# Strassen's block products for 16 of 22 input blocks of a down projection, with weight sums made by accumulating transfers

## The chip, the cores and the metric

One core of a Trainium2 chip runs the kernel. The metric is the device time of one execution in microseconds (us), the median of several. The engines are named as the profile names them: PE is TensorE's matmuls and PEld its weight loads (here the stationary operand of a matmul, which in this stage is an activation tile), DVE is VectorE, ACT is ScalarE, POOL is GpSimd and SP is SyncE. SP and POOL each issue transfers on a queue of their own.

## What is computed

A transformer-like block over 512 tokens of width 1024: an SSD branch and an attention branch are merged and added to x, and then comes a gated feed-forward network, whose last line is what the change is about.

```python
x = x + merged @ w_out[l]
h2 = rms_norm(x, norm2_g[l])
u = causal_dwconv(h2 @ w_up[l], ffn_conv_w[l], ffn_conv_b[l])
u_gate, u_val = jnp.split(u, 2, axis=-1)
x = x + (jax.nn.silu(u_gate) * u_val) @ w_down[l]
```

All inputs are float32. `w_down` is 2816 x 1024, so the down projection multiplies 512 x 2816 activations by it: 22 input blocks of 128 channels, two column halves of 512, four token tiles of 128.

## The kernel before

Every float32 operand of a product is split into a high part (`hi`, rounded to the matmul's format) and a low part (`lo`, the rest). A product of two blocks is then three matmuls: high x high, low activation x high weight, high activation x low weight.

Weights come in pieces of 512 KB in the order of a list, `pieces`. `load_piece` (L90) issues the load of the next on SP into one of three `raw` buffers; `make_piece` (L96) has ACT copy it to `whi` (L105) and DVE subtract to `wlo` (L106), three buffers each. A buffer is free when PE has done with the piece that held it. For the down projection a piece is two input blocks by one column half, `[128, 2, 512]`.

The activations stand in `act`, 22 blocks of `[128, 512]`, channels on partitions and tokens along the row. `split_act` (L1257) makes the high part on ACT and the low part on DVE, into `pre` for the first two blocks and into `asp` for the rest.

The up projection runs before, one block m of 22 after the other (loop at L1265). Its even blocks from 4 on (`fast`) already take Strassen's 7 products, with sums of weights made on POOL (`form`) and sums of activations in `sh`, `sl`. The last block, m = 21, is a plain one: 48 matmuls. During it the first two pieces of the down projection are loaded and made, and the first two activation blocks are split.

After it come the convolution of block 21 (`conv_a` on ACT, `conv_s` on DVE), its silu and product (`mul`, L1160), the load of the residual x into `x1b` (2 MB, L1376), and the down projection: `mm_tok` (L946) once for each column half. It takes four PSUM banks, one for each token tile, goes through the 11 pieces, and issues 24 matmuls for each: 4 token tiles x 3 terms x 2 blocks, with the activation tile `[128, 128]` stationary and the weights `[128, 512]` moving (L952). The last two pieces of a half are taken tile by tile, so that each bank ends at a time of its own; `store` then adds it into `x1b` on DVE (L1384) and SP stores 256 KB (L1385). The activations are split a second time for the second half.

PE's instructions are issued in the order written throughout. For DVE, ACT and POOL the written order holds from L1167 to the exit of `up_cm` at L1370; after it a planner sets the order. Each engine takes its instructions in order.

SBUF is two stacks. On the left, `pre` stays below `sums` (`sh`, `sl`, 32 KB a partition), `wx` and `gu`; on the right `down` takes the place of `h2` and `x1b` comes after it. A tile that takes another's place waits for that one's last reader.

Of the kernel before, what the change touches and what calls it, by code (L numbers as in the profile page):

```python
# [8 lines left out]
F32 = mybir.dt.float32  # L9
F32R = mybir.dt.float32r  # L10
AF = mybir.ActivationFunctionType
ALU = mybir.AluOpType
# [4 lines left out]
P = 128  # L17
# [17 lines left out]
NF = DFF // P  # L35
# [3 lines left out]
def kernel(  # L39
# [6 lines left out]
    nc = tc.nc  # L46
    x, out = x[0], out[0]
    w_in, w_ssd_proj, w_attn_proj, w_out, w_up, w_down = (
        w[0] for w in (w_in, w_ssd_proj, w_attn_proj, w_out, w_up, w_down))
# [4 lines left out]
    def pool(name, side="left", bufs=1):  # L54
        return tc.tile_pool(name=name, bufs=bufs, side=side, reuse_waits="tile")

    cp = ctx.enter_context(pool("const"))
    wp = ctx.enter_context(pool("weights"))
# [3 lines left out]
    def bank(tag, name):  # L62
        return pp.tile([P, 512], F32, tag=tag, name=name, bufs={"mm": 4, "tr": 2, "aux": 2}[tag])


    def chan_piece(w, c0, n, k0=0, nk=KD):
        return w[k0 * P:(k0 + nk) * P, c0:c0 + n].rearrange("(k p) c -> p k c", p=P)

    pieces = []
# [12 lines left out]
    pieces += [chan_piece(w_out, n * 512, 512, k, 2) for n in range(2) for k in range(0, KD, 2)]  # L82
    first_up = len(pieces)
    pieces += [chan_piece(w_up, i * DFF + m * P, P) for m in range(NF) for i in range(2)]
    pieces += [chan_piece(w_down, n * 512, 512, k, 2) for n in range(2) for k in range(0, NF, 2)]
    raws, made = [], []
    used = [0]
    marks = {}
# [1 line left out]
    def load_piece():  # L90
        n = len(raws)
        raw = wp.tile([P, pieces[n].shape[1], pieces[n].shape[2]], F32, tag="raw", name=f"raw{n}", bufs=3)
        nc.sync.dma_start(raw, pieces[n])
        raws.append(raw)

    def make_piece():  # L96
        n = len(made)
        if n == len(pieces):
            return
        if n == len(raws):  # L100
            load_piece()
        raw, shape = raws[n], list(raws[n].shape)
        hi = wp.tile(shape, F32R, tag="whi", name=f"whi{n}", bufs=3)
        lo = wp.tile(shape, F32R, tag="wlo", name=f"wlo{n}", bufs=3)
        nc.scalar.copy(hi, raw)  # L105
        marks["lo"] = nc.vector.tensor_sub(lo, raw, hi.bitcast(F32))  # L106
        made.append((hi, lo))

    def prefetch(n=2):
        while len(made) < min(used[0] + n, len(pieces)):  # L110
            make_piece()

    def next_piece(ahead=1):
        i = used[0]
        used[0] += 1
        while len(made) < min(i + 1 + ahead, len(pieces)):
            make_piece()
        return made[i]
# [690 lines left out]
    for g in range(8):  # L809
# [4 lines left out]
        banks = []  # L814
        for i in range(6):
            w = next_piece()
# [61 lines left out]
    for m2 in range(4):  # L878
        w = next_piece()
        for j in range(2):  # L880
            m = 2 * m2 + j
            ps = bank("mm", f"ps_ap{m}")
# [9 lines left out]
    with pool("ysplit") as sp:  # L892
# [14 lines left out]
        for m4 in range(2):  # L907
            pss = [bank("mm", f"ps_sp{m4}_{j}") for j in range(4)]
            for k2 in range(8):
                hi, lo = next_piece()  # L910
                ys = split_y(8 * m4 + k2)
                split_y(8 * m4 + k2 + 1)
                for j in range(4):
                    if j == 2:
                        prefetch()
                    cs = slice(j * P, (j + 1) * P)
                    for i, (w, xi) in enumerate(((hi, 0), (hi, 1), (lo, 0))):
                        for k in range(2):
                            nc.tensor.matmul(pss[j], w[:, k, cs], ys[k][xi],  # L919
                                             start=(k2 == 0 and i == 0 and k == 0),  # L920
                                             stop=(k2 == 7 and i == 2 and k == 1))
# [13 lines left out]
    act = actp.tile([P, NF, S], F32, tag="act", name="act")  # L935
# [10 lines left out]
    def mm_tok(xs, nk, name, fin, last, ahead=lambda k: None):  # L946
        pss = [bank("mm", f"ps_{name}{b}") for b in range(NT)]

        def part(b, k0, w):
            for j, (ww, i) in enumerate(((w[0], 0), (w[0], 1), (w[1], 0))):  # L950
                for k in range(2):
                    nc.tensor.matmul(pss[b], xs(k0 + k, i)[:, b * P:(b + 1) * P], ww[:, k, :],  # L952
                                     start=(k0 == 0 and j == 0 and k == 0),
                                     stop=(k0 == nk - 2 and j == 2 and k == 1))
        for k0 in range(0, nk - 2 * last, 2):
            w = next_piece()
            for b in range(NT):
                part(b, k0, w)
                if b == 1:
                    ahead(k0 + 2)  # L960
                    prefetch()
        ws = [next_piece(0) for i in range(last)]
        for i in range(1, last):
            ahead(nk - 2 * last + 2 * i)

        def ending(b):
            for i, w in enumerate(ws):
                part(b, nk - 2 * last + 2 * i, w)
            return pss[b]
        if fin is None:  # L970
            return ending
        prefetch(1)
        for b in range(NT):
            fin(b, ending(b))
# [3 lines left out]
    sums = n2.tile([P, NT, 2], F32, tag="sums", name="sums")  # L978
# [43 lines left out]
    H = 256  # L1022
# [116 lines left out]
    def conv_a(m, i):  # L1139
        if 0 <= m < NF:  # L1140
            if i == 0:
                facc[m] = gu.tile([P, S], F32, tag="facc", name=f"facc{m}", bufs=1)
            blk = m + NF * i
            nc.scalar.activation(act[:, m, :] if i else facc[m], (ga, ua)[i][m], AF.Identity,
                                 bias=sc[:, FB + blk:FB + blk + 1], scale=sc[:, FW + 88 + blk:FW + 89 + blk])
# [12 lines left out]
    def mul(m):  # L1158
        if 0 <= m < NF:
            nc.vector.tensor_mul(act[:, m, :], act[:, m, :], facc[m])  # L1160
# [6 lines left out]
    up_cm = tc.manual_schedule(engines={mybir.EngineType.DVE, mybir.EngineType.Activation, mybir.EngineType.Pool})  # L1167
# [9 lines left out]
    ps = ending(2)  # L1177
# [7 lines left out]
    ps = ending(3)  # L1185
# [69 lines left out]
    asp = {}  # L1255

    def split_act(k, p, tag, bufs):  # L1257
        t = p.tile([P, 2, S], F32R, tag=tag, name=f"{tag}{len(asp)}_{k}", bufs=bufs)
        nc.scalar.copy(t[:, 0, :], act[:, k, :])
        nc.vector.tensor_sub(t[:, 1, :], act[:, k, :], t[:, 0, :].bitcast(F32))  # L1260
        return t
# [3 lines left out]
    for m in range(2, NF):  # L1265
# [7 lines left out]
        else:  # L1273
            pss = [bank(t, f"ps_u{m}_{i}") for i, t in enumerate(("aux", "tr"))]
# [73 lines left out]
            asp[1] = split_act(1, pre, "pre", 2)  # L1348


    m = NF - 1
    h2_cm.__exit__(None, None, None)
    dn_cm = pool("down", side="right")
    dn = dn_cm.__enter__()
    fresh = {0, 1}

    def ahead(k):
        for i in (k, k + 1):
            if i < NF and i not in fresh:
                asp[i] = split_act(i, dn, "asp", 8)  # L1360
                fresh.add(i)

    ahead(2)
    conv_a(m, 1)
    conv_a(m, 0)
    conv_s(m, 1)
    conv_s(m, 0)
    silu_g(m)
    mul(m)
    up_cm.__exit__(None, None, None)  # L1370
    gu_cm.__exit__(None, None, None)
    wx_cm.__exit__(None, None, None)
    ss_cm.__exit__(None, None, None)
    xb_cm = pool("x1b", side="right")
    x1b = xb_cm.__enter__().tile([P, NT, D], F32, tag="x1b", name="x1b")
    nc.sync.dma_start(x1b, x1d.rearrange("(t p) d -> p t d", p=P))  # L1376

    def xs_a(k, i):
        return asp[k][:, i, :]

    def store(nh):
        def fin(b, ps):
            cs = slice(nh * 512, (nh + 1) * 512)
            nc.vector.tensor_add(x1b[:, b, cs], x1b[:, b, cs], ps)  # L1384
            nc.sync.dma_start(out[b * P:(b + 1) * P, cs], x1b[:, b, cs])  # L1385
        return fin

    mm_tok(xs_a, NF, "wd0_", store(0), 2, ahead)
    fresh.clear()
    ahead(0)  # L1390
    mm_tok(xs_a, NF, "wd1_", store(1), 2, ahead)
    xb_cm.__exit__(None, None, None)
    dn_cm.__exit__(None, None, None)
    pre_cm.__exit__(None, None, None)
    act_cm.__exit__(None, None, None)
# [28 lines left out]
```

## Time and profile before

| | |
|---|---|
| median of 3 runs | 1204.27 us (1204.27 to 1204.46) |
| the profiled execution | 1204.23 us, of which the span is 1202.3 us |
| PE busy | 1196.1 us of the span |
| DVE, ACT, POOL busy | 753.7, 575.4, 170.5 us |
| bytes moved | 138.95 MB, 116 GB/s on the mean |

The span goes from the first instruction to the last. "Busy" counts the time in which an engine has at least one instruction under way. In a list of groups, each row has the line of the kernel, the engine, the operation, the tile written and the tiles read, their shapes and the count; then busy time, the mean duration in ns, the idle time of the engine just before these instructions, and what ended most of it. In a list in order of time, a row starts with the start and the length in us.

### The profile page before, as it was taken

To read this page: it belongs to the slowest core of one execution; us is meant where nothing else is said; L and a number is where in the kernel's file an instruction comes from. 1 tells how busy PE (TensorE), PEld (TensorE's weight loads), DVE (VectorE), ACT (ScalarE), POOL (GpSimd) and SP (SyncE) were. 2 spreads that over 40 slices of the span, in tenths; PEclk is the share of its full clock that TensorE was granted. 3 is DMA by queue.
4 is the path that set the end of the run, shared out by engine and by line. 5 is a ranking of instruction groups with operands and counts; after the bars stand their busy time and mean duration, and the time that the engine had idled before them with its cause. 6 is when DMAs were issued, how large, how long until landed. Compare 5 with 4: busy or idle time off the path is not lost.

```text
span 1202.3 us, 15963 instructions
## 1 busy us (share of the span) xinstructions
PE 1196.1 (99%) x6316; PEld 997.8 (83%) x6316; DVE 753.7 (63%) x999; ACT 575.4 (48%) x890; POOL 170.5 (14%) x143
## 2 busy tenths in 40 slices
PE   9999999999999999999999999999999999999998
PEld 7877778987888888888888888888888989988887
DVE  6224544467789986877644354654788887885542
ACT  5434565467845657456433324433554445454331
POOL 1034422300000201101011000000223232400000
PEclk9999999999999999999999999999999999999999
DMA  5455544322646444434325332344333332334330
GB/s 187 123 124 128 114 103 107 91 66 74 184 124 200 122 134 124 123 97 115 87 72 144 119 103 90 105 142 157 123 108 103 105 107 85 109 95 168 112 116 35
DMA packets 174955, 138.95 MB, mean 116 GB/s; under 512 B 11552, under 2 KB 149584, under 8 KB 173857
## 3 DMA queue, kind: packets, MB, share of 16 engines
q1 hardware_dynamic: 172001, 131.35, 37.6%
q0 software_dynamic: 2880, 6.59, 2.4%
q8 instruction: 49, 0.80, 0.3%
q14 instruction: 25, 0.20, 0.1%
HBM read 133.22 MB, written 4.70 MB: 115 GB/s over the span
## 4 chain that ended last, share of the span: by engine, by line
PE 99%; ACT 0%; DVE 0%; issue 0%; POOL 0%; DVEq 0%
PE ps_ssd L145 22%; PE ps_qk L145 11%; PE ps_u L1282 10%; PE ps_wd L952 10%; PE ps_gate L145 7%; PE ps_sp L919 7%; PE ps_v L409 6%; PE ps_wo L952 3%; PE ps_ua L1108 2%; PE ps_uc L1108 2%; PE ps_ub L1108 2%; PE ps_u L145 2%; PE ps_ap L145 2%; PE ps_s L537 1%; PE ps_y L764 1%; PE ps_pv L579 1%
## 5 line engine op out<-in xcount | busy, mean ns | idle before, releaser
L106 DVE TENSOR_TENSOR wlo<-raw,whi 128x1024 fp32r<-128x1024 f32 x154 | 194.3, 1263 | 315.2 <-ACT whi L105 217.1
L105 ACT CAST whi<-raw 128x1024 fp32r<-128x1024 f32 x154 | 161.7, 1051 | 308.3 <-PE ps_ssd L145 63.1
L145 PE MATMUL ps_ssd<-hl,whi 128*128 128x512 f32 x384 | 102.9, 397 | 0.0
L145 PE MATMUL ps_ssd<-hh,whi 128*128 128x512 f32 x384 | 98.4, 398 | 0.0
L145 PE MATMUL ps_ssd<-hh,wlo 128*128 128x512 f32 x384 | 95.4, 390 | 0.0
L952 PE MATMUL ps_wd<-whi,asp 128*128 128x512 f32 x336 | 89.8, 389 | 0.0
L145 PEld LDWEIGHTS ps_ssd<-hh,wlo 128*128 128x128 f32 x384 | 72.1, 188 | 15.9
L145 PEld LDWEIGHTS ps_ssd<-hh,whi 128*128 128x128 f32 x384 | 70.6, 188 | 14.0 <-issue 0.2
L145 PEld LDWEIGHTS ps_ssd<-hl,whi 128*128 128x128 f32 x384 | 70.2, 188 | 14.1 <-issue 0.2
L952 PEld LDWEIGHTS ps_wd<-whi,asp 128*128 128x128 f32 x336 | 63.1, 188 | 13.1
L952 PE MATMUL ps_wd<-wlo,asp 128*128 128x512 f32 x168 | 51.7, 389 | 0.0
L556 ACT ACTIVATE s<-s,st 128x128 f32<-128x128 f32 (+1 forms) x96 | 39.8, 417 | 21.6 <-DVE st L550 15.7
L145 PE MATMUL ps_qk<-hh,whi 128*128 128x512 f32 x192 | 49.3, 398 | 0.0
L1156 ACT ACTIVATE facc<-facc 128x512 f32<-128x512 f32 x22 | 13.9, 632 | 71.7 <-DVE facc L52 71.6
L145 PE MATMUL ps_qk<-hl,whi 128*128 128x512 f32 x192 | 47.4, 389 | 0.0
L145 PE MATMUL ps_qk<-hh,wlo 128*128 128x512 f32 x192 | 47.4, 389 | 0.0
L1092 DVE TENSOR_TENSOR ulo<-rawup,uhi 128x1024 fp32r<-128x1024 f32 x31 | 43.5, 1404 | 5.2 <-ACT uhi L1086 5.2
L778 POOL TENSOR_TENSOR sq<-sq 128x512 f32<-128x512 f32 x8 | 12.4, 1550 | 240.5 <-ACT sq L775 240.5
L145 PEld LDWEIGHTS ps_qk<-hh,whi 128*128 128x128 f32 x192 | 35.0, 188 | 12.1 <-issue 3.8
L1282 PE MATMUL ps_u<-h2h,uhi 128*128 128x512 f32 x176 | 43.7, 390 | 0.0
L1282 PE MATMUL ps_u<-h2h,ulo 128*128 128x512 f32 x176 | 43.5, 389 | 0.0
L1282 PE MATMUL ps_u<-h2l,uhi 128*128 128x512 f32 x176 | 43.5, 389 | 0.0
(321 smaller groups left out, 2530.0 us busy)
## 6 DMA issues: line engine op xcount, KB each, us to landing
raw<-in_w_in_dram SPq DMA_DIRECT2D x100, 512.0 KB
rawup<-in_w_up_dram SPq DMA_DIRECT2D x40, 512.0 KB
raw<-in_w_down_dram SPq DMA_DIRECT2D x22, 512.0 KB
bc<-scr_a SPq DMA_DIRECT2D x8, 1024.0 KB
raw<-in_w_ssd_proj_dram SPq DMA_DIRECT2D x16, 512.0 KB
hrb<-scr_q POOLq DMA_DIRECT2D x12, 512.0 KB, 6.7
eb<-scr_e SPq DMA_DIRECT2D x16, 256.0 KB
raw<-in_w_out_dram SPq DMA_DIRECT2D x8, 512.0 KB
```

Source lines behind the costliest of these rows:

```text
L105: nc.scalar.copy(hi, raw)
L106: marks["lo"] = nc.vector.tensor_sub(lo, raw, hi.bitcast(F32))
L145: nc.tensor.matmul(ps[:, t0:t0 + nt], a[:, k, c:c + n], b[:, k, t0:t0 + nt], start=(i == 0), stop=(i == total - 1))
L409: nc.tensor.matmul(pss[b], tok(g, kq * 2 + k, b, xx), w[:, k, :], start=(kq == 0 and j == 0 and k == 0), stop=(kq == 3 and j == 2 and k == 1))
L556: nc.scalar.activation(s[:, o:o + nk * P], s[:, o:o + nk * P], AF.Exp, bias=st[:, q, 0, 2 * j + h:2 * j + h + 1], accum_out=st[:, q, 1, 2 ...
L778: nc.gpsimd.tensor_add(sq[:, 0, :], sq[:, 0, :], sq[:, 1, :])
L919: nc.tensor.matmul(pss[j], w[:, k, cs], ys[k][xi], start=(k2 == 0 and i == 0 and k == 0), stop=(k2 == 7 and i == 2 and k == 1))
L952: nc.tensor.matmul(pss[b], xs(k0 + k, i)[:, b * P:(b + 1) * P], ww[:, k, :], start=(k0 == 0 and j == 0 and k == 0), stop=(k0 == nk - 2 and ...
L1092: nc.vector.tensor_sub(lo, source(m, x), hi.bitcast(F32))
L1108: nc.tensor.matmul(ba[m][bk][:, c * H:(c + 1) * H], a[:, k, :], b[:, k, :], start=(i == 0), stop=(i == 11))
L1156: nc.scalar.activation(facc[m], facc[m], AF.Silu)
L1282: nc.tensor.matmul(pss[i], a[:, k, :], b[:, k, :], start=(n == 0), stop=(n == 23))
```

## The change

The input blocks 0 to 5 stay plain (three pieces for each column half: A_0 to A_2 for columns 512 to 1023, B_0 to B_2 for columns 0 to 511). The blocks 6 to 13 (X) and 14 to 21 (Y) are the two halves of the inner dimension, the tokens are halved in 256 and 256, the columns in 512 and 512. Of this 2 x 2 by 2 x 2 block product the form with 7 products is used: P1, P2, Q3, Q4, Q5, Q6, Q7, each in four pieces (_0 to _3) of two blocks. One such piece is 12 matmuls: 2 token tiles x 3 terms x 2 blocks, of the same shapes as before.

- The sums of weights are held in eight tiles of 512 KB, `sums[0]` and `sums[1]`, four each. SP loads a quarter of `w_down` into each. A product is made from the tile as it stands (copy on ACT, subtraction on DVE, into the same three `whi` and `wlo` buffers), and then POOL issues a transfer that adds another quarter to the tile. `sums[0]` goes through P1, Q5, Q6 and Q4, three additions for each of its four tiles; `sums[1]` through Q3 and Q7, one addition: 16 accumulating transfers of 512 KB. P2's weights come as plain pieces.
- The sums of activations, S1 to S4, four tiles each, are made on DVE (`form_s`), 16 of `[128, 512]`. For each piece of a product its activations are split anew into one of four `asq` buffers, a copy on ACT and a subtraction on DVE of `[128, 512]`: 28 in all. The plain blocks' splits are made once and serve both column halves.
- The order of the 34 pieces is written out in `ORDER`. Each is prepared two places ahead (`prepare`), and behind it, in the order of DVE, stand the sums and adds that `EXTRA` lists for the place.
- The PSUM banks: A and B use the four `mm` banks one after the other. P1 and, on top of it, Q6 use the two `tr` banks; Q5 and, on top, Q3 the two `aux` banks, which then serve Q7. P2 and Q4 go on top of B. Where a bank is added to an output block in between, the next product on it comes after that. 24 adds of a bank into `x1b` (or subtractions from it) take the place of 8. The eight stores stay.
- The written order of DVE, ACT and POOL now holds to the end: the exit of `up_cm` stands behind the down projection.
- SP's queue has the four loads of `sums[0]`, one piece, `x1b`, and the four loads of `sums[1]`, in this order; `sums` takes the place of `sh` and `sl`.

The diff, cut to its core:

```diff
-    pieces += [chan_piece(w_down, n * 512, 512, k, 2) for n in range(2) for k in range(0, NF, 2)]
+    pieces += [chan_piece(w_down, n * 512, 512, k, 2) for k, n in
+               ((0, 1), (2, 1), (4, 1), (0, 0), (2, 0), (14, 0), (4, 0), (16, 0), (18, 0), (20, 0))]
...
-    ahead(2)
+    X0, Y0 = 6, 14
+    split_plain(1)
     conv_a(m, 1)
...
     mul(m)
-    up_cm.__exit__(None, None, None)
...
+    for i in range(4):
+        nc.sync.dma_start(sums[0][i], quarter(0, i, 0))
+    load_piece()
     nc.sync.dma_start(x1b, x1d.rearrange("(t p) d -> p t d", p=P))
+    for i in range(4):
+        nc.sync.dma_start(sums[1][i], quarter(1, i, 1))
+    CHAIN = {"P1": (0, (0, 1)), "Q5": (0, (1, 1)), "Q6": (0, (1, 0)), "Q4": (0, None),
+             "Q3": (1, (0, 1)), "Q7": (1, None)}
+    NEEDS = {"Q5": "S1", "Q6": "S2", "Q3": "S4", "Q7": "S3"}
...
+    def prepare(x):
...
+            j, more = CHAIN[k]
+            hi = wp.tile([P, 2, 512], F32R, tag="whi", name=f"dhi{x}", bufs=3)
+            lo = wp.tile([P, 2, 512], F32R, tag="wlo", name=f"dlo{x}", bufs=3)
+            nc.scalar.copy(hi, sums[j][i])
+            nc.vector.tensor_sub(lo, sums[j][i], hi.bitcast(F32))
+            if more:
+                nc.gpsimd.dma_start(sums[j][i], quarter(more[0], i, more[1]), accum_op=ALU.add)
...
+        t = dn.tile([P, 2, 2, H], F32R, tag="asq", name=f"asq{x}", bufs=4)
+        nc.scalar.copy(t[:, 0], src)
+        nc.vector.tensor_sub(t[:, 1], src, t[:, 0].bitcast(F32))
...
+    ORDER = """A_0 A_1 P1_0 P1_1 P1_2 P1_3 Q5_0 Q5_1 A_2 Q5_2 Q5_3 Q6_0 Q6_1 Q3_0 B_0 Q6_2 Q3_1 Q6_3 Q3_2 Q3_3
+               B_1 Q7_0 Q7_1 P2_0 Q7_2 Q7_3 B_2 Q4_0 P2_1 Q4_1 Q4_2 Q4_3 P2_2 P2_3""".split()
...
+    EXTRA = {
+        "A_0": [forms("S1_3")], "A_1": [forms("S3_0")], "P1_0": [forms("S3_1")],
+        "P1_1": [forms("S3_2")], "P1_2": [forms("S3_3")],
+        "A_2": [adds(("c", 0, 0, 0, 1, 0), ("c", 1, 1, 0, 1, 0))],
+        "Q5_3": [adds(("A", 0, 0, 1, 1, 0))],
+        "Q6_0": [adds(("A", 1, 1, 1, 1, 0), ("a", 0, 2, 1, 1, 0))],
+        "Q6_1": [adds(("a", 1, 3, 1, 1, 0), ("A", 2, 2, 1, 1, 0))],
+        "Q3_0": [adds(("A", 3, 3, 1, 1, 0))],
...
+    for n, x in enumerate(ORDER):
+        if n + 2 < len(ORDER):
+            prepare(ORDER[n + 2])
+        if x == "P2_2":
+            for b in range(2):
+                products("P2_2", b)
+                products("P2_3", b)
+                add(banks["B"][b], b, 0, 1, 1)
+            break
+        products(x)
+        for f in EXTRA.get(x, ()):
+            f()
+    up_cm.__exit__(None, None, None)
```

More of the change, by code (lines that the diff above doesn't have):

```diff
@@ L1354, with split_plain @@
     dn = dn_cm.__enter__()
[L1355 to L1361, printed above, removed]
-    ahead(2)
+    X0, Y0 = 6, 14
+    def split_plain(i):
+        for k in (2 * i, 2 * i + 1):
+            if k not in asp:
+                asp[k] = split_act(k, dn, "asp", 4)
+    split_plain(1)
     conv_a(m, 1)
@@ L1373 @@
     ss_cm.__exit__(None, None, None)
+    chain_cm = pool("chain")
+    chp = chain_cm.__enter__()
     xb_cm = pool("x1b", side="right")
     x1b = xb_cm.__enter__().tile([P, NT, D], F32, tag="x1b", name="x1b")
-    nc.sync.dma_start(x1b, x1d.rearrange("(t p) d -> p t d", p=P))
[L1378 to L1391, printed above, removed]
+    def quarter(k, i, n):
+        return chan_piece(w_down, n * 512, 512, (X0, Y0)[k] + 2 * i, 2)
+    def inputs(k, i, t):
+        k0 = (X0, Y0)[k] + 2 * i
+        return act[:, k0:k0 + 2, t * H:(t + 1) * H]
+    sums = [[chp.tile([P, 2, 512], F32, tag=f"c{j}{i}", name=f"c{j}_{i}") for i in range(4)] for j in range(2)]
+    diffs = [chp.tile([P, 2, H], F32, tag=f"s{i}", name=f"s_{i}") for i in range(4)]
@@ new lines, with form_s @@
+    for i in range(4):
+        nc.sync.dma_start(sums[0][i], quarter(0, i, 0))
+    load_piece()
+    nc.sync.dma_start(x1b, x1d.rearrange("(t p) d -> p t d", p=P))
+    for i in range(4):
[3 more added lines that the diff above has]
+    NEEDS = {"Q5": "S1", "Q6": "S2", "Q3": "S4", "Q7": "S3"}
+    formed, ready = set(), {}
+    def form_s(x):
+        k, i = x.split("_")
+        i = int(i)
+        formed.add(x)
+        a11, a12, a21, a22 = (inputs(k2, i, t) for t in range(2) for k2 in range(2))
+        if k == "S1":
+            nc.vector.tensor_sub(diffs[i], a21, a22)
+        elif k == "S2":
+            nc.vector.tensor_sub(diffs[i], diffs[i], a11)
+        elif k == "S3":
+            nc.vector.tensor_sub(a21, a11, a21)
+        else:
+            nc.vector.tensor_add(diffs[i], diffs[i], a12)
@@ new lines, in prepare @@
+    def prepare(x):
+        k, i = x.split("_")
+        i = int(i)
+        if k in "AB":
+            if k == "A":
+                split_plain(i)
+            if len(made) == len(raws):
+                load_piece()
+            make_piece()
+            if len(raws) < len(pieces):
+                load_piece()
+            ready[x] = made[-1]
+            return
+        if k in NEEDS and f"{NEEDS[k]}_{i}" not in formed:
+            form_s(f"{NEEDS[k]}_{i}")
+        if k == "P2":
+            make_piece()
+            if len(raws) < len(pieces):
+                load_piece()
+            w = made[-1]
+        else:
+            j, more = CHAIN[k]
[5 more added lines that the diff above has]
+                nc.gpsimd.dma_start(sums[j][i], quarter(more[0], i, more[1]), accum_op=ALU.add)
+            w = hi, lo
+        src = {"P1": inputs(0, i, 0), "P2": inputs(1, i, 0), "Q4": inputs(1, i, 1), "Q7": inputs(0, i, 1)}.get(k, diffs[i])
+        t = dn.tile([P, 2, 2, H], F32R, tag="asq", name=f"asq{x}", bufs=4)
+        nc.scalar.copy(t[:, 0], src)
+        nc.vector.tensor_sub(t[:, 1], src, t[:, 0].bitcast(F32))
+        ready[x] = w, t
@@ new lines, in add @@
+    def add(ps, b, n, sign=1, last=False):
+        o = x1b[:, b, n * 512:(n + 1) * 512]
+        (nc.vector.tensor_add if sign > 0 else nc.vector.tensor_sub)(o, o, ps)
+        if last:
+            nc.sync.dma_start(out[b * P:(b + 1) * P, n * 512:(n + 1) * 512], o)
+    ORDER = """A_0 A_1 P1_0 P1_1 P1_2 P1_3 Q5_0 Q5_1 A_2 Q5_2 Q5_3 Q6_0 Q6_1 Q3_0 B_0 Q6_2 Q3_1 Q6_3 Q3_2 Q3_3
+               B_1 Q7_0 Q7_1 P2_0 Q7_2 Q7_3 B_2 Q4_0 P2_1 Q4_1 Q4_2 Q4_3 P2_2 P2_3""".split()
+    SETS = {"A": "A", "P1": "c", "Q6": "c", "Q5": "a", "Q3": "a", "B": "B", "Q7": "b", "P2": "B", "Q4": "B"}
@@ new lines, with products @@
+    TAGS = {"A": ("mm", 4), "B": ("mm", 4), "a": ("aux", 2), "b": ("aux", 2), "c": ("tr", 2)}
+    banks, begun = {}, set()
+    def products(x, only=None):
+        k = x.split("_")[0]
+        bs = SETS[k]
+        if bs not in banks:
+            banks[bs] = [bank(TAGS[bs][0], f"ps_d{bs}{b}") for b in range(TAGS[bs][1])]
+        pss = banks[bs]
+        if k in "AB":
+            w = ready[x]
+            i = int(x.split("_")[1])
+            todo = [(b, pss[b], lambda j, q, b=b: asp[2 * i + q][:, j, b * P:(b + 1) * P]) for b in range(4)]
+        else:
+            w, t = ready[x]
+            o = 2 if k == "Q4" else 0
+            todo = [(b, pss[b + o], lambda j, q, b=b: t[:, j, q, b * P:(b + 1) * P]) for b in range(2)]
+        final = {"A_2": 1, "P1_3": 1, "Q5_3": 1, "Q6_3": 1, "Q3_3": 1, "Q7_3": 1, "Q4_3": 1, "P2_3": 1}
+        for b, ps, xs in todo:
+            if only is not None and b != only:
+                continue
+            n = 0
+            for wi, j in ((0, 0), (0, 1), (1, 0)):
+                for q in range(2):
+                    nc.tensor.matmul(ps, xs(j, q), w[wi][:, q, :], start=ps.name not in begun, stop=x in final and n == 5,
+                                     skip_group_check=k in ("Q6", "Q3"))
+                    begun.add(ps.name)
+                    n += 1
@@ new lines, in adds, with run, forms @@
+    def adds(*l):
+        def run():
+            for bs, b, blk, n, sign, last in l:
+                add(banks[bs][b], blk, n, sign, last)
+        return run
+    def forms(*l):
+        return lambda: [form_s(x) for x in l]
+    EXTRA = {
[6 more added lines that the diff above has]
+        "Q3_0": [adds(("A", 3, 3, 1, 1, 0))],
+        "B_1": [adds(("a", 0, 0, 1, 1, 0), ("a", 1, 1, 1, 1, 0), ("c", 0, 0, 1, -1, 1), ("c", 1, 1, 1, -1, 1))],
+        "Q7_1": [adds(("c", 0, 2, 0, 1, 0))],
+        "P2_0": [adds(("c", 1, 3, 0, 1, 0))],
+        "B_2": [adds(("c", 0, 2, 1, -1, 0), ("c", 1, 3, 1, -1, 0), ("b", 0, 2, 1, -1, 1))],
+        "Q4_0": [adds(("b", 1, 3, 1, -1, 1))],
+        "P2_1": [adds(("b", 0, 2, 0, 1, 0))],
+        "Q4_1": [adds(("b", 1, 3, 0, 1, 0))],
+        "Q4_3": [adds(("B", 2, 2, 0, 1, 1), ("B", 3, 3, 0, 1, 1))],
+    }
@@ new lines @@
+    for i in range(3):
+        form_s(f"S1_{i}")
+    ready["A_0"] = made[-2]
+    ready["A_1"] = made[-1]
+    for n, x in enumerate(ORDER):
[11 more added lines that the diff above has]
+    up_cm.__exit__(None, None, None)
@@ L1392 @@
     xb_cm.__exit__(None, None, None)
+    chain_cm.__exit__(None, None, None)
     dn_cm.__exit__(None, None, None)
```

## The prediction

> **What bounds the kernel now.** First the page: the span, and the share of each engine.
>
> ```profile
> span 1202.3 us, 15963 instructions
> PE 1196.1 (99%) x6316; PEld 997.8 (83%) x6316; DVE 753.7 (63%) x999; ACT 575.4 (48%) x890; POOL 170.5 (14%) x143
> PEclk9999999999999999999999999999999999999999
> ```
>
> TensorE (PE) is never without work, at full clock. Then the chain that ended last, from the end of the last fast up-projection block on:
>
> ```profile
> 1066.37 1.41 PE ps_ud L1108 x12
> 1067.78 10.91 PE ps_u L1282 x48
> 1078.69 119.69 PE ps_wd L952 x528
> 1198.38 0.02 issue
> 1198.41 0.69 DVE x1b L1384
> ```
>
> The whole down projection is one piece of PE work without a gap, 528 matmuls in 119.69 us: 0.2267 us each. Behind it stand one VectorE (DVE) add and the last store, 1202.3 - 1198.38 = 3.9 us. So a matmul taken away is worth 0.2267 us, if operands still arrive in time. Third, the same stretch (from 1040 us on) grouped by line and form, columns count, busy us, mean ns, idle before and who ended it:
>
> ```profile
> L106 DVE TENSOR_TENSOR wlo<-raw,whi 128x1024 fp32r<-128x1024 f32 x22 | 26.9, 1224 | 47.9 <-ACT whi L105 46.7 <-PE ps_u L1282 1.2
> L1260 DVE TENSOR_TENSOR asp<-act,asp 128x512 fp32r<-128x512 f32 x42 | 26.9, 684 | 0.0
> L105 ACT CAST whi<-raw 128x1024 fp32r<-128x1024 f32 x22 | 23.2, 1054 | 60.6 <-PE ps_wd L952 60.4 <-DVE ulo L1092 0.2
> L1384 DVE TENSOR_TENSOR x1b<-x1b,ps_wd 128x512 f32<-128x512 f32 x8 | 5.5, 685 | 16.2 <-PE ps_wd L952 16.2
> ```
>
> ScalarE (ACT) waits 60.4 us for PE to free a weight buffer, DVE 46.7 us for ACT: both are fed by PE's pace, not PE by theirs. That slack is what the change spends.
>
> **What it takes from PE.** Six plain blocks remain: 3 pairs x 2 column halves x 24 = 144 matmuls. Of the other 16 the plain form needs 8 products of 48 (8 blocks x 2 token tiles x 3 terms), the new one 7: 336. Together 480, so 48 fewer, all of the same 128x512 shape: 48 x 0.2267 = **10.88 us**, the most there is to win. PE's schedule from 1078.69 is then counted in steps of one product piece, 12 matmuls = 2.72 us; a plain piece is two steps. In the order of the diff, P1_0 to P1_3 start at steps 4 to 7, Q5_0 at 8, Q5_1 at 9, Q5_2 at 12, Q5_3 at 13, Q6_0 at 14, Q6_1 at 15, Q3_0 at 16, Q7_0 at 26, Q7_3 at 30, the last pair at 38, the end at 40 (108.8 us).
>
> **What it adds to ACT and DVE.** The pace of both is best read where they work back to back, in order of time:
>
> ```profile
> 1084.31 0.74 DVE L52 SCALAR_TENSOR_TENSOR facc<-ps_u,sc,facc 128x510 f32<-128x510 f32 x1
> 1084.96 1.22 DVE L106 TENSOR_TENSOR wlo<-raw,whi 128x1024 fp32r<-128x1024 f32 x1
> 1086.10 0.69 DVE L1160 TENSOR_TENSOR act<-act,facc 128x512 f32<-128x512 f32 x1
> 1086.70 2.49 DVE L1260 TENSOR_TENSOR asp<-act,asp 128x512 fp32r<-128x512 f32 x4
> 1090.24 1.22 DVE L106 TENSOR_TENSOR wlo<-raw,whi 128x1024 fp32r<-128x1024 f32 x1 [1.05 <-ACT whi L105]
> 1091.38 1.28 DVE L1260 TENSOR_TENSOR asp<-act,asp 128x512 fp32r<-128x512 f32 x2
> ...
> 1089.15 1.05 ACT L105 CAST whi<-raw 128x1024 fp32r<-128x1024 f32 x1 [3.34 <-PE ps_wd L952]
> 1090.11 1.14 ACT L1259 CAST asp<-act 128x512 fp32r<-128x512 f32 x2
> ```
>
> From start to start a 128x1024 subtraction costs DVE 1.14, a 128x512 one 0.60 us (2.49 for four, the ends overlap); ACT's copies cost 0.96 and 0.52. DVE then has 32 wlo x 1.14 = 36.5, 28 new input splits x 0.60 = 16.8, 4 plain splits 2.4, 16 input sums 9.6, 24 adds into x1b (8 before) 14.4, and 3.4 for the last up block: 83 us in 108.8, or 76%. ACT has 32 x 0.96 + 28 x 0.52 + 2.1 = 47 us. The second splitting of the inputs (22 of the 42 asp) goes; it lay under PE and gains nothing. On average both fit; the cover is PE's work, and if it failed, each missing DVE us would be a us of the end.
>
> A piece is ready 1091.38 + 0.68 - 1089.15 = 2.9 us after ACT starts on it (copy, wlo, input's low part). With three weight buffers that start comes when PE leaves the piece three before, two steps = 5.4 us ahead: 2.5 us to spare for one add or sum (0.60) and more. At the start: in the trace the last up block's product is done at 1086.70, with two weight subtractions and two splits among it that the new order leaves out or puts later; I take 1084.5. Three sums (1.8), then P1_0's wlo ends at 1087.5 and its split at 1088.1; it is due at 1078.69 + 4 x 2.72 = 1089.6. P1_1 to P1_3 follow at 1090.4, 1092.8, 1095.1 against 1092.3, 1095.0, 1097.7. So no stall from DVE here: **0**. Keeping the written order of ACT, DVE and POOL to the end costs nothing by itself: what is queued behind a waiting copy on ACT is only the next copies, but behind a waiting wlo on DVE stand the adds that free PSUM banks, which matters below. On SP the stores of the first finished blocks stand ahead of the loads for B_2 and later; these have 10 us and more until used. The end is as before: last matmul, one add, one store, 3.9 us.
>
> **What it adds to the DMAs.** 8 loads of 512 KB on SP and 16 accumulating transfers of 512 KB on POOL's queue take the place of 12 loads; x1b stays. No accumulating transfer is in the trace of before. Its nearest rows, a window of the down projection (last columns DMA share, GB/s), the same size on POOL's queue beside other traffic, a small one there, and that queue's total:
>
> ```profile
> 1090.00:1100.00 10.00, 10.00 (x46) 8.29 (x45) 4.85 (x6) 3.34 (x6) 0.00 (x0) 1.00 0.77 296
> ```
>
> ```profile
> L511 POOL DMA_DIRECT2D hrb<-scr_q x12: 622/630/646, 82.1 to 225.5; - x12
> DMA to landing us min/median/max: 4.9/6.7/8.6
> ```
>
> ```profile
> q0 software_dynamic: 2880, 6.59, 2.4%
> scr_q<-hs POOLq DMA_DIRECT2D x24, 4.0 KB, 2.3
> ```
>
> A plain load runs at 296/0.77 = 384 GB/s while it runs: 0.524 MB is 1.37 us of all DMA engines. The 4 KB one shows the fixed part, 2.3 us. POOL's own queue took 2.4% of 1202.3 us for 6.59 MB: 2.30 us for 0.524 MB. Call T the engine time of one accumulating transfer. It must read the addend and the old sum and write the new one. The low end is 1.37 (reading costs nothing extra), the high end 4.6 (POOL's 2.30, doubled); I take 2 x 1.37 = 2.74, nearest to the plain load of the same shape in the same stage, because I see no reason for POOL's contended rate here, but keep 4.6 for the range.
>
> The Trainium skill, page "Collectives: The Full Stack", section "The bandwidth ceiling: the fold count and why AG ≠ RS ≠ AR", says that an add inside a DMA is slower because it reads two sources, by a measured 1.93; an estimate by it is T = 2.64 and a sum 0.2 us lower than mine. No run here shows it yet.
>
> Where the transfers are due: Q5_0 starts at 1078.69 + 8 x 2.72 = 1100.5, so its copy must start by 1097.6; likewise Q5_1 1100.3, Q5_2 1108.4, Q5_3 1111.1, Q6_0 1113.9, Q6_1 1116.6. From about 1085 SP's queue carries x1b (2 MB) and four sums, 8 x 1.37 = 11 us. In the window from 109 to 122 us both queues were at work and took like shares for like bytes:
>
> ```profile
> q1 hardware_dynamic: 2464, 1.18, 44.6%
> q0 software_dynamic: 416, 1.07, 34.1%
> ```
>
> So I give POOL's queue half while both are busy. First transfer: 1087.5 + 2.3 + 2 x 2.74 = 1095.3, in time (1097.6). The second queues behind it: 5.5 us more, 1100.9, due 1100.3: **0.6 us** late. Third and fourth, with SP's burst over at 1103, about 1106 and 1109 (due 1108.4, 1111.1); fifth and sixth 1112 and 1115 (1113.9, 1116.6). Later ones come one per 2.7 to 3.3 us and have 17 us and more. POOL waits in each for DVE's wlo; nothing else is queued on POOL. The wait of Q5_1 and a late copy hold up DVE's queue with it, and the two adds that must empty the Q5 banks before Q3_0 at step 16 stand there; at 2.74 I count that within the 0.6.
>
> The Trainium skill, page "DMA: Bandwidth & Descriptors", section "Queues, rings and completion order", has each engine change between queues packet by packet, not by time; with POOL's packets twice as long it would get two thirds, the second transfer would land near 1098 and the stall be nothing: sum 10.88, 1193.35. The two rows above fit either.
>
> **Sum.** The profiled execution took 1204.23 us with a span of 1202.3 (1.9 around it); the median of the three runs is 1204.27, 0.04 above. 1204.23 - 10.88 + 0.6 = 1193.95, say **1194.0**.
>
> **Rivals.** (a) T between 2.9 and 3.8: each 0.3 us of T puts the second transfer 1.2 us and Q3_0's bank some 0.6 us later. At T = 3.3 that is near 4 us of stall: 1204.23 - 10.88 + 4 = 1197.4. For it: hrb's median of 6.7 us, not 4.9. (b) Slower: the accumulating transfers become the bound. The sixteenth must land by Q7_3's copy, 1078.69 + 30 x 2.72 - 2.9 = 1157.4; from 1088.4 that is 69 us, of which SP's queue needs 8 x 1.37 + 6 x 1.37 = 19. Of the 50 left each may have 3.1 us before the end moves, and beyond it 16 us are lost per us of T: the gain is gone at T = 3.1 + 10.88/16 = 3.8. At the high end, 4.6: 16 x 0.8 = 12.8, 1217. Against it: the queue's 2.30 includes its small transfers and time shared with the other queue. (c) DVE becomes the bound. Its subtractions grew where POOL worked beside it, in order of time:
>
> ```profile
> 1047.96 1.93 DVE L1092 TENSOR_TENSOR ulo<-rawup,uhi 128x1024 fp32r<-128x1024 f32 x1
> 1052.30 1.22 DVE L1092 TENSOR_TENSOR ulo<-t,uhi 128x1024 fp32r<-128x1024 f32 x1
> ...
> 1048.77 2.27 POOL L1070 TENSOR_TENSOR t<-rawup,t 128x512 f32<-128x512 f32 x1
> ```
>
> 1.93 with POOL at work, 1.22 without: if writing descriptors did this to 16 subtractions, 16 x 0.7 = 11 us of DVE, of which its 25 us of slack take the most; with 4 of them in the dense start, 3 us are lost: 1197. Against it, hrb's 0.63 us on POOL is short. (d) The gain is whole: 1193.35 (T under 2.5).
>
> **Chances.** My forecast with (d), T to 2.9: 0.45, with a range of its own of 1193.0 to 1195.5. (a) 0.24, (c) 0.07, both faster unless stalls reach 8.5 us (0.03 of them come out within 0.2%). (b) 0.24, of which 0.03 ends within 0.2%. A change of under 0.2% (2.4 us) can't be told from none. Faster 0.73, the same 0.06, slower 0.21. The range goes from 1192.8 (all of the gain and 0.5 us) to 1212 (T = 4.3); of (b) some 0.14 lies above.
>
> **What would show it.** PE: 480 matmuls at 0.227 us; the stage's piece of the chain 108.8 us long plus stalls. Landing of the accumulating transfers: 6 to 10 us for the first four, under 6 later, is T = 2.74; 12 and growing is (b), with ACT's whi waiting for the DMA before Q5 and again before Q7. PE waiting before Q5_1 and Q3_0 only is (a). wlo's mean over 1.4 us is (c). The forecast is wrong if T is over 3 or if a buffer I took for free (the sums' memory is released by PE at 1067.8) comes late.

## The result, and the profile after

The changed kernel takes **1193.87 us** (median of four runs, 1192.88 to 1194.38) against 1204.37 for the kernel before: a ratio of 0.9908, with a 95% interval of 0.9894 to 0.9921. The forecast was 1194.0. The profiled execution took 1193.57 us. Its page, the lines that answer to those of before:

```profile
span 1191.8 us, 15944 instructions
PE 1185.9 (100%) x6268; PEld 989.3 (83%) x6268; DVE 784.7 (66%) x1033; ACT 583.7 (49%) x892; POOL 186.0 (16%) x159
PEclk9999999999999999999999999999999999999999
```

PE has 48 instructions fewer and, in this stage, still no idle time. The end of the chain of waits, in order of time:

```profile
1068.48 10.91 PE ps_u L1283 x48
1079.39 10.88 PE ps_dA L1484 x48
1090.27 10.88 PE ps_dc L1484 x48
1101.15 5.44 PE ps_da L1484 x24
...
1163.71 24.49 PE ps_dB L1484 x108
1188.20 0.02 issue
1188.22 0.69 DVE x1b L1453
```

Every piece is a whole number of 12 matmuls at 2.72 us; no other engine and no "issue" stands between them, in the rows left out here too. The down projection as one window (columns: us, then busy us and instructions of PE, PEld, DVE, ACT, POOL, then granted clock, DMA share, GB/s), first after, then before:

```profile
1079.39:1188.20 108.81, 108.80 (x480) 89.74 (x479) 84.65 (x108) 52.42 (x67) 19.31 (x16) 1.00 0.67 155
```

```profile
1078.69:1198.38 119.69, 119.68 (x528) 98.75 (x527) 57.44 (x74) 43.59 (x64) 0.00 (x0) 1.00 0.31 108
```

119.69 - 108.81 = 10.88 us, the whole of 48 matmuls. DVE went from 57 to 85 us, the DMAs' share from 0.31 to 0.67, and PE does not notice. Where the transfers came nearest to being noticed is on ACT, in order of time, at the copies for Q5_0 and Q5_1:

```profile
1096.82 1.05 ACT L1440 CAST dhiQ<-c 128x1024 fp32r<-128x1024 f32 x1 [2.67 <-DMA c<-in_w_down_dram]
1097.77 0.61 ACT L1447 CAST asqQ<-s 128x512 fp32r<-128x512 f32 x1
1099.41 1.06 ACT L1440 CAST dhiQ<-c 128x1024 fp32r<-128x1024 f32 x1 [1.03 <-DMA c<-in_w_down_dram]
```

ACT waits for the first two accumulating transfers, 3.7 us together, and for no later one. With the 0.7 us by which the stage began later, these copies were due at 1098.3 and 1101.0: 1.5 and 1.6 us to spare.

A smaller margin is on DVE, at the adds that empty the two banks of Q5 for Q3_0:

```profile
1120.73 0.68 DVE L1453 TENSOR_TENSOR x1b<-x1b,ps_da 128x512 f32<-128x512 f32 x1
...
1122.47 0.68 DVE L1453 TENSOR_TENSOR x1b<-x1b,ps_da 128x512 f32<-128x512 f32 x1
```

In the chain Q3_0 starts at 1122.91, 1.5 us after the first add ends. Its seventh matmul, the first on the second bank, comes at 1122.91 + 6 x 0.227 = 1124.27, 1.1 us after the second add ends at 1123.15.

### The profile page after: what moved, and what is told of

It reads as the page before. It is cut to its first block, busy times and chain, and to the rows that moved or that the text cites. A ratio compares the mean times of both kernels' runs of the same rounds, so it can differ in the third digit from the quotient of the medians.

```text
span 1191.8 us, 15944 instructions
## 1 busy us (share of the span) xinstructions
PE 1185.9 (100%) x6268; PEld 989.3 (83%) x6268; DVE 784.7 (66%) x1033; ACT 583.7 (49%) x892; POOL 186.0 (16%) x159
## 4 chain that ended last, share of the span: by engine, by line
PE 99%; ACT 1%; DVE 0%; issue 0%
PE ps_ssd L146 22%; PE ps_qk L146 11%; PE ps_u L1283 10%; PE ps_gate L146 7%; PE ps_sp L920 7%; PE ps_v L410 5%; PE ps_wo L953 3%; PE ps_dB L1484 3%; PE ps_ua L1109 2%; PE ps_uc L1109 2%; PE ps_ub L1109 2%; PE ps_u L146 2%; PE ps_da L1484 2%; PE ps_dc L1484 2%; PE ps_ap L146 2%; PE ps_s L538 1%
## 5 line engine op out<-in xcount | busy, mean ns | idle before, releaser
L107 DVE TENSOR_TENSOR wlo<-raw,whi 128x1024 fp32r<-128x1024 f32 x142 | 181.3, 1277 | 274.5 <-ACT whi L106 175.4
L106 ACT CAST whi<-raw 128x1024 fp32r<-128x1024 f32 x142 | 149.0, 1050 | 255.8 <-PE ps_ssd L146 60.8
L1093 DVE TENSOR_TENSOR ulo<-rawup,uhi 128x1024 fp32r<-128x1024 f32 x31 | 46.1, 1487 | 5.2 <-ACT uhi L1087 5.2
L146 PEld LDWEIGHTS ps_qk<-hl,whi 128*128 128x128 f32 x192 | 36.0, 188 | 7.6
L146 PEld LDWEIGHTS ps_qk<-hh,wlo 128*128 128x128 f32 x192 | 36.0, 188 | 7.5
L52 DVE SCALAR_TENSOR_TENSOR xst<-ps_ssd,sc,xst 128x511 f32<-128x511 f32 (+2 forms) x48 | 35.7, 744 | 6.4 <-ACT xst L678 5.9
```

The source lines that it names most:

```text
L52: nc.vector.scalar_tensor_tensor(o, a, s, b, op0=op0, op1=op1)
L146: nc.tensor.matmul(ps[:, t0:t0 + nt], a[:, k, c:c + n], b[:, k, t0:t0 + nt], start=(i == 0), stop=(i == total - 1))
L1093: nc.vector.tensor_sub(lo, source(m, x), hi.bitcast(F32))
```

## The experiments

**The changed kernel again.** No edit.

> The changed kernel once more, beside the others. Theory (all of the gain is 48 matmuls fewer, and nothing waits): the down projection's part of the chain is 480 matmuls in 108.8 us, without a gap, and the time is 1193.9 us within 0.8. Rival (the gain is in part a lucky profile, and stalls come in other executions): the stage is longer than 109.5 us here, and the time is 1195 or more.

1193.66 us (1192.84 to 1194.7), ratio 0.9907 (0.9892 to 0.9923). The end of its chain:

```profile
1079.78 10.88 PE ps_dA L1484 x48
...
1188.59 0.02 issue
```

108.81 us again: PE does not wait in this execution either, and the rival falls.

**The kernel before, profiled again.** No edit.

> The kernel before the change, profiled once more, to see how much the start of the down projection moves between executions of one kernel. Theory (the 0.7 us by which the changed kernel reached it later come from the first 30 us of the execution and differ from one execution to the next): it starts between 1078.7 and 1080.0 us and lasts 119.7 us. Rival (the change itself delays what goes before): 1078.7 again.

```profile
1079.23 119.69 PE ps_wd L952 x528
1198.93 0.02 issue
```

The stage lasts 119.69 us to the hundredth, and starts 0.54 us later than in the first profile of the same kernel. Over all kernels here, whose work for PE up to the stage is the same, the start lies between 1078.69 and 1079.81 us. Most of the 0.7 us in the changed kernel's profile is there long before the changed code: in the chain, a piece of 48 matmuls of `ps_qk` starts at 36.38 us in the first profile of the kernel before, at 36.94 in this one, and at 36.94 in the changed kernel's. So I put the 0.7 us down to the spread between executions and not to the change; the runs' own spread of some 1.5 us is of the same size.

**Only the order.** The kernel before, with the line that ends the written order moved:

```diff
     mul(m)
-    up_cm.__exit__(None, None, None)
     gu_cm.__exit__(None, None, None)
...
     mm_tok(xs_a, NF, "wd1_", store(1), 2, ahead)
+    up_cm.__exit__(None, None, None)
```

> The kernel before the change, with one line moved: the written order of DVE, ACT and POOL holds to the end, as in the changed kernel, and there are no block products of Strassen's. Theory (PE sets the end and is never without work, so the order of the others is worth nothing): 1204.3 us, within 0.5. Rival (part of the 10.4 us comes from the order, not from the matmuls): below 1203 us.

1206.32 us (1205.75 to 1208.29) against 1204.51, ratio 1.0015 (1.0006 to 1.0023). Neither theory: it is slower. The chain:

```profile
1079.53 59.85 PE ps_wd L952 x264
1139.38 0.02 issue
1139.41 0.04 DVE x1b L1383
...
1140.01 1.30 DVE asp L1260 x2
...
1141.36 59.48 PE ps_wd L952 x261
```

Between the two column halves PE stands 1139.38 to 1141.36, 2.0 us: the last half's first splits of `asp` are written behind the last adds of the first half, and DVE now takes them in this order; the planner had put them earlier: in the profile of before 24 are done by 1130.7 us, four more than the first half needs. So the order by itself gives none of the gain; it can cost. That `ORDER` and `EXTRA` are what keeps it from costing in the changed kernel is my reading, and no run here takes them away.

**The adding left out.** The transfers overwrite the tile, so the weight sums are left out.

```diff
-                nc.gpsimd.dma_start(sums[j][i], quarter(more[0], i, more[1]), accum_op=ALU.add)
+                nc.gpsimd.dma_start(sums[j][i], quarter(more[0], i, more[1]))
```

> The 16 transfers on POOL's queue write the new quarter over the tile and do not add it, so the weight sums are left out and the products are of single quarters; all instructions and bytes from DRAM stay. Theory (an adding transfer costs the DMA engines 178 ns for each 2048-byte packet where a plain one costs 84, as it reads two sources; PE does not wait for it in either case): a packet takes 84 to 90 ns, the rate of POOL's queue alone rises from 205 to over 350 GB/s, landing falls to 4 to 5.5 us, and the time stays at 1193.9 us. Rival (the adding is no dearer; the rate of 205 GB/s is that of POOL's queue): 178 ns and 205 GB/s stay.

1193.16 us (1192.89 to 1193.92): no difference that this can tell, as the theory has it. What one transfer costs, from the rows of tile `c` (issue on POOL in ns, min/median/max, and landing), first with the adding, then without:

```profile
L1443 POOL DMA_DIRECT2D c<-in_w_down_dram x16: 1194/1203/1290, 1089.2 to 1138.8; - x16
DMA to landing us min/median/max: 5.7/7.5/8.4
```

```profile
L1443 POOL DMA_DIRECT2D c<-in_w_down_dram x16: 724/724/780, 1089.6 to 1139.1; - x16
DMA to landing us min/median/max: 3.9/4.0/5.4
```

The adding makes the issue 0.48 us longer and the best landing 1.8 us. The queue's own time from 1105 to 1124 us, first with the adding, then without:

```profile
q0 software_dynamic: 1628, 3.14, 93.9%
```

```profile
q0 software_dynamic: 723, 2.63, 44.6%
```

That is 17.8 us for 3.14 MB (5.7 us a MB) against 8.5 us for 2.63 MB (3.2), a ratio of 1.8. The expected packet of 84 to 90 ns can't be read off, since the plain transfers go in packets of another size; the rate in the fullest slices of that window is 388 GB/s, and the rival's 205 is excluded. That adding makes the transfers dearer is shown; why it does (reading two sources, or something else in the adding) is not.

**Half as much again for the DMAs.**

```diff
                 nc.gpsimd.dma_start(sums[j][i], quarter(more[0], i, more[1]), accum_op=ALU.add)
+                nc.gpsimd.dma_start(spare[i], quarter(more[0], i, more[1])[:, :1, :], accum_op=ALU.add)
```

The four `spare` tiles are set to zero by POOL before the stage.

> Each accumulating transfer of 512 KB is followed on the same queue by one of 256 KB into a spare tile that no engine reads: one and a half times the work for the DMA engines, the same sums. Theory (the transfers have 1.5 us to spare at Q5_0 and Q5_1 and the DMA engines are busy all the time from 1088 to 1146 us, 2.55 us for each transfer): the waits grow, and PE loses 1 to 3 us, most of it before Q3_0: 1195 to 1197 us. The prediction's rule for transfers as the bound (T = 2.74 x 1.5 = 4.1, gain gone at 3.8): 1204.2 + 16 x 0.3 = 1209 us. Rival (the transfers have much room): 1193.9, no difference.

1196.66 us (1195.53 to 1197.18), ratio 0.9931 (0.9918 to 0.9943): 3.0 more than the changed kernel on the same chip, in the theory's range; the prediction's rule, with its own T, said 1209. Who waited for whom, count and longest last:

```profile
ACT dhiQ L1443 <- DMA c<-in_w_down_dram: 18.4, 7, 4.4
PE ps_da L1488 <- DVE x1b L1457: 1.7, 1, 1.7
```

ACT's wait for the transfers is 18.4 us instead of 3.7, and of that PE feels little: most of it at the place that was named, Q3_0 (`ps_da`), where the Q5 bank is freed by an add that stands behind a late preparation on DVE.

**Twice as much for the DMAs.** As above, with `[:, :2, :]`.

> As with half, but the extra transfer has 512 KB: twice the work for the DMA engines. Theory (from the changed kernel's own rows: 5.1 us for a pair, issued from 1089 us on, Q7's weights wait for the backlog): PE stands some 20 us, mostly before Q7, and the time is 1211 to 1217 us, slower than before the change. The prediction's rule for transfers as the bound, with T = 5.1: 1204.2 + 16 x 1.3 = 1225 us. Rival (the transfers have much room): within 2 us of 1193.9.

1217.98 us (1215.85 to 1218.14), ratio 1.0105 (1.0092 to 1.0119): the change is now a loss. 24.3 us more than the changed kernel, a little over the theory's range and well under the rule's 1225. In the chain the DMAs stand by name, and the stage ends 24.4 us later than in the changed kernel:

```profile
1110.52 21.70 DMA spare<-in_w_down_dram
...
1145.58 15.06 DMA spare<-in_w_down_dram
...
1161.91 19.42 DMA c<-in_w_down_dram
...
1188.03 24.52 PE ps_dB L1488 x108
1212.55 0.02 issue
```

The mean rate in forty slices from 1060 to 1216 us shows what the engines can do when only such transfers are queued:

```profile
GB/s 88 185 137 381 370 391 87 368 235 207 205 207 206 258 210 208 204 208 205 228 241 208 206 210 249 218 205 207 230 258 244 81 107 27 71 67 0 0 200 69
```

Plain loads run at 370 to 390 (near the start of the row), accumulating ones at 205 to 208: 0.524 MB/0.206 = 2.54 us each. One wait is of the experiment's own making, as a row of the waits has it:

```profile
POOL spare L1447 <- DMA spare<-in_w_down_dram: 26.5, 3, 11.9
```

POOL waited for a spare tile's last transfer to land, and the next transfers were issued only after that; a kernel with dearer transfers would not have this wait. But the DMA engines did not stand meanwhile. Their busy share in the same forty slices, in tenths, is nine or more in every slice from 1087 to 1181 us:

```profile
DMA  2559993999999999999999999999999430210051
```

So the trace gives no sign that POOL's waits lengthen the stage. A run without them was not made.

**More work for DVE.**

```diff
-        nc.vector.tensor_sub(t[:, 1], src, t[:, 0].bitcast(F32))
+        for _ in range(2):
+            nc.vector.tensor_sub(t[:, 1], src, t[:, 0].bitcast(F32))
```

> Each of the 28 low parts of the products' activations is computed twice: 28 x 0.60 = 16.8 us more of DVE in the down projection (85 busy us become 101 of 108.8), nothing else. Theory (DVE has room on the whole but 1.5 to 2 us in the dense stretch before Q3_0, where adds that free PSUM banks stand behind the preparations): PE loses 1 to 4 us, before Q3_0 and around Q5_1: 1195 to 1198 us. Rival (DVE is already the bound, and each us of it is one of the end): 1210 us. Rival (DVE's slack takes it all): 1193.9 us.

1196.04 us (1195.53 to 1197.66), ratio 0.9929 (0.9917 to 0.9942). By the window of the stage DVE is busy 102.7 us instead of 84.65, 18.1 us more, of which 2.6 reach the stage's end. The stage starts and ends, with one piece near the first gap and the first half of Q3_0 between, at

```profile
1079.81 10.88 PE ps_dA L1485 x48
...
1096.59 3.04 PE ps_dc L1485 x12
...
1125.34 1.62 PE ps_da L1485 x6
...
1191.20 0.02 issue
```

111.39 us instead of 108.81; PE's small gaps are spread from P1_2 (12 matmuls in 3.04 us instead of 2.72) to Q3_0. On the whole DVE is not the bound, and it has no room left where the pieces are dense.

**The sums on POOL.** The quarters are loaded by SP and added by POOL.

```diff
-                nc.gpsimd.dma_start(sums[j][i], quarter(more[0], i, more[1]), accum_op=ALU.add)
+                extra = chp.tile([P, 2, 512], F32, tag="extra", name=f"extra{x}", bufs=4)
+                nc.sync.dma_start(extra, quarter(more[0], i, more[1]))
+                nc.gpsimd.tensor_add(sums[j][i], sums[j][i], extra)
```

> The 16 quarters are loaded by SP into four tiles of their own, and POOL adds them to the weight sums as 128x1024 tensor additions; no accumulating transfer is left. Theory (the sums as such fit anywhere, but POOL's additions slow the subtractions of DVE, which went from 1.22 to 1.93 us beside POOL, and DVE has little room before Q3_0): POOL is busy 16 x 2.8 = 45 us more, DVE's subtractions beside it take 0.5 us or more longer, and PE loses 2 to 10 us: 1196 to 1204 us. Rival (POOL is idle and its additions are free; the transfers need not add): 1193.9 us within 0.8.

1212.67 us (1211.82 to 1213.7), ratio 1.0065 (1.0052 to 1.0077): 19 us lost against the changed kernel, beyond the theory's range; its mechanism shows, its size was too small. Groups of the stage, mean ns of one second after the bar:

```profile
L1412 DVE TENSOR_TENSOR act<-act 128x512 f32<-128x512 f32 x4 | 11.5, 2880 | 0.0
L1414 DVE TENSOR_TENSOR s<-s,act 128x512 f32<-128x512 f32 x4 | 10.3, 2580 | 0.0
L1410 DVE TENSOR_TENSOR s<-s,act 128x512 f32<-128x512 f32 x4 | 8.1, 2033 | 0.0
L1455 DVE TENSOR_TENSOR x1b<-x1b,ps_dc 128x512 f32<-128x512 f32 x8 | 5.2, 680 | 0.0
...
L1445 POOL TENSOR_TENSOR c<-c,extraQ 128x1024 f32<-128x1024 f32 x12 | 33.3, 2774 | 24.6 <-DVE dloQ L1441 24.6
```

The input sums on DVE, 0.69 us in the changed kernel, take 2.0 to 2.9 us on the mean: about as long as one of POOL's additions, 2.77. They do not share, they wait it out, as one pair shows in order of time:

```profile
1092.60 2.78 POOL L1445 TENSOR_TENSOR c<-c,extraP 128x1024 f32<-128x1024 f32 x1 [1.76 <-DVE dloP L1441]
1093.05 2.88 DVE L1412 TENSOR_TENSOR act<-act 128x512 f32<-128x512 f32 x1
```

The addition ends at 1095.38 and the sum 0.55 us later. The adds that read one operand from PSUM keep their 0.68. The Trainium skill, page "SBUF — State Buffer", section "Who interferes with whom", says that a DVE instruction with two SBUF inputs contends with a GpSimd instruction that reads SBUF, that one with a single SBUF input does not (outside modes that use two ports), and calls the shared ports an exclusive lock. The trace agrees on all three. I had priced the collision at 0.5 us from one row of before (1.93 against 1.22); here nearly each addition meets the sum that is queued behind the same preparation. DVE is busy 115.2 us of the stage instead of 84.65, and without a gap from 1085 to 1163 us, so that it is the bound there: of its 30.5 us more 18.9 reach the stage's end.

## Why the prediction was right, point by point

**48 matmuls, 10.88 us: right**, to 0.01 us, in two profiles each of before and after (119.69, 119.69, 108.81, 108.81).

**DVE and ACT fit: right.** Forecast 83 and 47 us of busy time by the distance from start to start, measured 84.65 and 52.42 by the window, which counts the last instruction of each burst at its full length; for ACT I had also left out the three instructions of the last up block, 2 us. P1_0's subtraction was forecast to end at 1087.5 and ended near 1088.6, 0.7 of it the later start. Where the margin was smallest, at Q3_0's second bank, 1.1 us were left. That the issuing of transfers on POOL slows DVE (rival c) is refuted by the groups of the stage after:

```profile
L1441 DVE TENSOR_TENSOR dloQ<-c,dhiQ 128x1024 fp32r<-128x1024 f32 x20 | 24.5, 1224 | 14.4 <-ACT dhiQ L1440 14.4
```

1224 ns, as before the change, beside 16 issues of 1.2 us on POOL. One of P1's subtractions lay under an issue for its first 0.8 us (1089.77 to 1090.99 us, the issue 1089.24 to 1090.53) and took 1.22 us.

**The written order at no cost: right here, but not by itself.** The prediction said that keeping it costs nothing by itself. In the kernel before it cost 2.0 us of PE's time between the column halves; in the changed kernel PE shows no gap.

**0.6 us of stall at Q5_1: wrong, it is 0.** Three terms behind it were off. T is 2.54 us, not 2.74: 1.86 times the 1.37 of a plain load, not 2. That adding is what costs is shown by the run without it; that it costs because two sources are read stays argued. The Trainium skill, page "Collectives: The Full Stack", section "The bandwidth ceiling: the fold count and why AG ≠ RS ≠ AR", gives 1.93 for sums made in collectives; the trace is a little below it. The issue costs 1.2 us on POOL, not 0.63, which works the other way. And SP's burst was half of what I assumed. The working had slips of its own, too: 1095.3 + 5.5 is 1100.8, which makes the stall 0.5, and T = 2.64 would have lowered the sum by 0.4, not 0.2. SP's queue in order of time:

```profile
1068.51 1.91 SPq L1390 DMA_DIRECT2D c<-in_w_down_dram  x4
1070.46 2.31 SPq L1394 DMA_DIRECT2D c<-in_w_down_dram  x4
1072.87 2.79 SPq L94 DMA_DIRECT2D raw<-in_w_down_dram  x2
1085.74 0.37 SPq L1392 DMA_DIRECT2D x1b<-x1d  x1
```

The four loads of `sums[1]` (L1394) stand behind `x1b` in the code, but SP is not among the engines whose written order is kept, and they were issued 15 us ahead of it. Only the 2 MB of `x1b` were left when the first accumulating transfer came, and the rate from 1088 us on (forty slices of 0.43 us) shows them pass before it:

```profile
GB/s 376 337 424 386 424 434 405 424 434 424 313 217 198 198 198 212 198 198 198 202 212 202 188 164 159 178 202 193 183 174 198 202 198 217 212 188 212 207 193 212
```

424 GB/s until 1092.3, then 200. So whether the queues share by halves or by packets can't be told from this. The first landing was forecast at 1095.3 and seen by ACT at 1096.8, the second at 1100.9 and seen at 1099.4. Landing came out near the sign that was given for T = 2.74: medians of 8.0 us for the six issued up to 1105 us, then 6.0 and 5.8.

**The sum: right, with errors that cancel by luck.** The profile's span is 1079.39 + 108.81 + 3.6 = 1191.8. Against the forecast the stage has 0.6 us less stall, and this execution came to it 0.7 us later, which is spread between executions; the end behind PE's last matmul, 3.6 us and not 3.9, takes most of the rest. The agreement with the median to 0.1 us is closer than the reasoning deserves; to 0.6 us it is earned.

**Rival (b), transfers as the bound: the mechanism right, the point where the loss begins misplaced.** With half as much again a transfer and its extra take 1.5 x 2.54 = 3.81 us and cost 3.0 us; the rule gives 1193.35 + 16 x 0.71 = 1204.7 for that T, 8 more than measured. With twice as much they take 5.08 us and cost 24.3. Between the two that is 21.3/1.27 = 17 us per us, against the 16 of the rule; as the first loss arises mostly at Q3_0 and the second mostly at Q7 (`ps_db`), this slope is rough. With 16 the second point puts the start of the loss at 5.08 - 24.3/16 = 3.6, not 3.1, and the gain is gone near 4.2, not 3.8. The rule took the traffic of SP's queue as 19 us in that stretch; with the loads of `sums[1]` done before, 5.5 us of it were not there, which is 0.34 us for each of 16 and most of the difference.

## What to carry to other kernels

Where one engine is without a gap, work taken from it is worth its full time as long as what is put on the others arrives: list, for each thing moved, when it is issued, when it is due, and what else uses its path, and look for the smallest difference. Here sums made by transfers cost 1.9 loads' time on the DMA engines and 1.2 us of POOL's issuing each, and nothing on DVE; the same sums on POOL made DVE wait for them and turned a gain of 10 us into a loss of 8. An edge that shows as 1.5 us to spare on ACT and 1.1 on DVE, and as nothing on PE, is worth testing with more load before the next thing is moved onto it: half as much again cost 3 us, twice as much 24.

## What the runs showed of the hardware that I had not expected

Issuing an accumulating transfer takes POOL 1.20 us where a plain one of the same 512 KB takes 0.72. A DVE sum of two SBUF operands that meets a POOL addition is not slowed in proportion but ends some 0.55 us after the addition does: 2.88 us instead of 0.69 where it came 0.45 us behind the addition's start. And the start of the last stage moves by 1.1 us (1078.69 to 1079.81) between executions of kernels whose work for PE up to it is the same, 0.54 us of it between two of one kernel, while the stage itself repeats to 0.01 us.
